# SSM table batches in finer steps beside the first feed-forward, and Toeplitz rows stored by one DMA per group

## The chip, the cores and the metric

One core of a Trainium2 chip runs the whole layer as one program. The metric is the device time of one execution in microseconds. The engines are TensorE (PE, matrix products), VectorE (DVE), ScalarE (ACT), GpSimd (POOL) and SyncE (SP), whose queue issues nearly all DMAs. Each works off its own list in order; they meet at semaphores.

## The reference

One layer on 1024 tokens of width 1024, float32:

```python
h = modulate(rms_norm(x, ffn1_norm), sh1, sc1)
x = x + 0.5 * g1 * swiglu(h, ffn1_w_gate, ffn1_w_up, ffn1_w_down)     # first feed-forward
h = modulate(rms_norm(x, mix_norm), sh2, sc2)
b, c, v, u = split(h @ w_in)
y_conv = short_conv_mixer(b, c, v, conv_w)
y_ssm = s5_mixer(u, lambda, log_dt, b, c, d, glu_w, glu_b)            # 32 groups, 64 states, 16 channels
x = x + g2 * (concat(rms_norm(y_conv), rms_norm(y_ssm)) @ w_out)
h = modulate(rms_norm(x, ffn2_norm), sh3, sc3)
x = x + 0.5 * g3 * swiglu(h, ffn2_w_gate, ffn2_w_up, ffn2_w_down)     # second feed-forward
return rms_norm(x, final_norm)
```

The shifts, scales and gates sh, sc, g are nine vectors, silu(cond) @ w_mod + b_mod. The state space model (SSM) `s5_mixer` is a diagonal recurrence over the tokens; the kernel does it in blocks of TAU = 8 tokens, with tables that depend on the weights alone: a block-Toeplitz matrix `mk` (what eight tokens do to each other), `mi` (tokens to state), `mo` (state to tokens) and the rotors `co` and `si`.

## The kernel before, in words

**First feed-forward.** The 22 column tiles of the gate and up matrices are taken two at a time, as groups fa0 to fa10. Groups 1 to 10 are formed by `seven`: seven products of blocks of weights and activations in place of eight. A block has a gate half (g) and an up half (u), each of four `mm3`; an `mm3` is three matmuls of 128x512 (high and low parts of a float32 split). So a group has 14 halves of 12 matmuls. The products gather in six PSUM banks per group, named B, C and A with g or u, as `fa4gB`. Bank B takes the first, third, fifth and seventh block, each added to what is there, and between them DVE or ACT reads it: the result of the fifth block is read by the DVE instructions `fa4gc` and `fa4uc`, before the seventh may start. Bank C takes the second and the fourth block, read by `fa4gu` and `fa4uu`; bank A the sixth (`fa4gt`, `fa4ut`). `fa4X`, `fa4Y`, `fa4Z`, `fa4W` are the group's products and their combinations, which SP stores as `kept4X` and so on.

**Weights.** Blocks come from DRAM to `raw` tiles (three; SP), some have a second one added by a DMA that POOL issues. ACT rounds them to `w` (high part), DVE subtracts (low part, `w<-raw,w`).

**Side work.** `clock.tick()` runs after each `mm3`, and every `clock.period` ticks the generator `side1` is advanced to its next `yield`. It forms combinations of the activations (`combos1`), the SSM base (`ssm_base`, period 4.5), and then, with period BATCH_PERIOD = 5.5, eight batches (`ssm_batch`) of four SSM groups. A batch loads its parameters `prm`, makes `bb`, `cl` and `bl` on DVE, stores `mo`, makes the rotors `rot` and `rott` and stores them, multiplies `cl` and `bl` on PE (`kp`, eight matmuls of 16x128) and transposes `bl` (`tp`), copies both on ACT (`kc`, `mi`), and stores `mi` and the Toeplitz rows from `kc`. `gate1` yields once if a product of `w_mod` is pending: 24 tiles `wm` of 512 KB are loaded into two buffers in turn, and DVE reduces each against silu(cond) (`mod_vector`), which makes the vectors g1, sc2 and sh2.

**What sets the order.** The code is written in this interleaved order, but past the start of the program a scheduler lays out each engine's list, by program order among what it takes to be ready. An instruction may so stand well ahead of its place in the code; the `wm` products do. At run time each list is strictly in order.

**Toeplitz rows.** `mk_d` is (batch, 128 rows, 4 groups x 128). Row block t (16 rows) has t x 16 zeros and then the first 128 - 16 t columns of `kc`. `ssm_base` stores the zeros, 7 blocks x 8 batches = 56 DMAs; a batch stores its rows in 8 DMAs of 64 pieces, from 512 bytes a piece down to 64.

**After it.** `down7` and `last_parts` finish the feed-forward; the mixer follows, where `out_loads` loads `mk` and `mo` of batch b + 1 after the matmuls of batch b, and `states` and `outputs` use them (`px`, `yy`).

Of the kernel before, what the change touches and what calls it, by code (L numbers as in the profile page):

```python
# [13 lines left out]
F32 = mybir.dt.float32  # L14
F32R = mybir.dt.float32r
I32 = mybir.dt.int32
AF = mybir.ActivationFunctionType
ALU = mybir.AluOpType
# [3 lines left out]
P = 128  # L22
# [9 lines left out]
CH = 16  # L32
TAU = 8
# [7 lines left out]
NB = 8  # L41
GB = G // NB
# [186 lines left out]
def hymba_layer(ctx: ExitStack, tc, x_d, xt_d, wm1_d, wmod_d, gu1_d, gs1_d, ds1_d, wl1_d, win_d, wout_d, glu_d, gu2_d, gs2_d, wd2_d, ds2_d, wl2_d, cols_d, cond_d, lam_d, bc_d, out_d):  # L229
# [228 lines left out]
    def mod_fetch(home):  # L458
        if share[0]:
            share[0] -= 1  # L460
            n, b, i = later.pop(0)
            r = home(f"wm{n}_{b}_{i}")
            SP.dma_start(r, wmod_d[n - 2, b, :, i, :])
            fetched.append((n, 2 * b + i, r))
# [327 lines left out]
    st = t2k("st")  # L792
# [211 lines left out]
    mk_d = scratch.tile([NB, P, GB * P], F32, name="mk_d")  # L1004
# [28 lines left out]
    def ssm_base(sb, sb1):  # L1033
# [130 lines left out]
        mk4 = mk_d[:].rearrange("b p (g c) -> p b g c", g=GB)  # L1164
        for t in range(1, TAU):
            for b in range(NB):
                SP.dma_start(
                    mk4[t * CH : (t + 1) * CH, b, :, 0 : t * CH],
                    zero[:, 0 : t * CH].unsqueeze(1).to_broadcast([CH, GB, t * CH]),
                )  # L1170
            yield
        ssm.update(q=qq, tabs=tabs, base=baset, step=step, lam=lam)

    def ssm_batch(b):
        bp = bps[0]
        gs = slice(b * GB, (b + 1) * GB)
        prm = bp.tile([P, 4, GB, CH], F32, tag="prm", name=f"prm{b}")
        SP.dma_start(prm[:], bc_d[b])
# [3 lines left out]
        p1, p2, e1, e2 = ssm["tabs"]  # L1182

        def bt(name):
            return bp.tile([P, 576], F32, tag="bt", name=name, bufs=4)

        def comb(dst, n, lam, src, op, nm):

            t = bt(nm)[:, : GB * n * CH].rearrange("p (g n c) -> p g n c", g=GB, n=n)
            la = [a[:, 0:n, gs].rearrange("p n g -> p g n").unsqueeze(3).to_broadcast([P, GB, n, CH]) for a in lam]  # L1190
            sc = [a.unsqueeze(2).to_broadcast([P, GB, n, CH]) for a in src]
            V.tensor_tensor(out=dst, in0=la[0], in1=sc[0], op=ALU.mult)
            V.tensor_tensor(out=t, in0=la[1], in1=sc[1], op=ALU.mult)
            yield
            V.tensor_tensor(out=dst, in0=dst, in1=t, op=op)

# [3 lines left out]
        SP.dma_start(mo_d[b].rearrange("p (g m) -> p g m", g=GB), cl4[:, :, 1:9, :].rearrange("p g n c -> p g (n c)"))  # L1200
        bl = bt(f"bl{b}")
        bl4 = bl[:, :512].rearrange("p (g n c) -> p g n c", g=GB, n=8)
        yield from comb(bl4, 8, (e1, e2), (bb[:, 0], bb[:, 1]), ALU.add, f"blt{b}")
        if b >= 2:
            yield from gate1()

        def v3(a):
            return a[:, :512].rearrange("p (g m i) -> p g m i", g=GB, m=8)
# [3 lines left out]

        def rotors():

            r, t = bt(f"rot{b}"), bt(f"rott{b}")
            V.tensor_tensor(out=v3(r), in0=st[0], in1=bs[0], op=ALU.mult)
            V.tensor_tensor(out=v3(t), in0=st[1], in1=bs[1], op=ALU.mult)
            yield
            V.tensor_tensor(out=r[:, :512], in0=r[:, :512], in1=t[:, :512], op=ALU.add)
            A.activation(t[64:128, :512], r[64:128, :512], AF.Copy, scale=-1.0)  # L1220
            for half in (slice(0, 64), slice(64, 128)):
                SP.dma_start(co_d[b, half], r[0:64, :512])
            SP.dma_start(si_d[b, 0:64], r[64:128, :512])
            SP.dma_start(si_d[b, 64:128], t[64:128, :512])

        yield from rotors()
        yield

# [8 lines left out]
        if b >= 2:  # L1237
            yield from gate1()
            yield from gate1()
            yield from gate1()  # L1240
        kc = bt(f"kc{b}")
        kc3 = kc[:CH, :512].rearrange("p (g m) -> p g m", g=GB)
        A.copy(kc[:CH, :512], kp[:])
        for g in range(GB):
            V.scalar_tensor_tensor(
                out=kc3[:, g, 0:CH], in0=ident[:CH, :CH], scalar=ssm["lam"][:CH, 3, b * GB + g : b * GB + g + 1], in1=kc3[:, g, 0:CH], op0=ALU.mult, op1=ALU.add
            )
        mk3 = mk_d[b].rearrange("p (g m) -> p g m", g=GB)
        for t in range(TAU):
            SP.dma_start(mk3[t * CH : (t + 1) * CH, :, t * CH :], kc3[:, :, : P - t * CH])  # L1250
        mi = bt(f"mi{b}")
        A.copy(mi[:, :512], tp[:])
        SP.dma_start(mi_d[b], mi[:, :512])
        yield


    def gate1():

        if fetched:
            mod_tile(mod_home)  # L1260
            yield
# [30 lines left out]
    def side1():  # L1292
        yield from combos1()
        clock.period = 4.5
        sb = side_open.enter_context(tc.tile_pool(name="sb", bufs=1, side="right"))
        with tc.tile_pool(name="sb1", bufs=1, side="right") as sb1:
            yield from ssm_base(sb, sb1)
        clock.period = BATCH_PERIOD
        bps.append(side_open.enter_context(tc.tile_pool(name="bp", bufs=1, side="right")))
        mod_home.pool = side_open.enter_context(tc.tile_pool(name="wmp", bufs=1, side="right"))  # L1300
        share[0] = MODS[1]
        for _ in range(2):
            mod_fetch(mod_home)
        for b in range(NB):
            yield from ssm_batch(b)
# [22 lines left out]
    BATCH_PERIOD = 5.5  # L1328
# [495 lines left out]
```

## Time and profile before

| | us |
|---|---|
| runs (three) | 1685.75, 1690.64, 1691.35; median 1690.64 |
| profiled execution | 1691.52, of which the span is 1689.7 |
| PE busy | 1657.2, 98% of the span |
| DVE busy | 1065.5, 63% |
| ACT busy | 676.8, 40% |
| DMA moved | 340.21 MB, mean 201 GB/s |

The rows in the prediction are of these kinds. A row of the page's first part has an engine's busy time, its share of the span and its instructions. A row by stretch has from:to, its length, and for PE, PEld (weight loads), DVE, ACT and POOL the busy time and (x) the instructions, then the granted TensorE clock (1.00 is full), the share of the DMA engines' time and GB/s. A row of a time line has start, duration, engine (SPq is SP's queue, issuing), line, operation and tiles out<-in, shapes and count; in brackets stand the idle time ahead of it and what ended it. A row of waits has who waited for whom, total us, times, the longest. A row of one tile's instructions has min/median/max duration in ns and the first and last start.

### The profile page before, as it was taken

How to read it: one execution, taken by the hardware profiler on the slowest of the kernel's cores; microseconds unless marked ns; L12 is line 12 of the kernel's file. 1: busy time of each engine (PE TensorE's matmuls, PEld its weight loads, DVE VectorE, ACT ScalarE, POOL GpSimd, SP SyncE). 2: the span in 40 equal slices, each digit the busy share in tenths (PEclk: the TensorE clock that was granted, in tenths of full speed). 3: DMA queues.
4: the chain of work that ended last, by engine and by line, in shares of the span. 5: the costliest groups of instructions: out<-in, count | busy, mean ns of one | idle time of the engine just before them, and what ended most of it. 6: DMA issues, size and time to landing. Idle time of an engine off the chain costs nothing.

```text
span 1689.7 us, 20647 instructions
## 1 busy us (share of the span) xinstructions
PE 1657.2 (98%) x7521; PEld 1364.8 (81%) x7521; DVE 1065.5 (63%) x1581; ACT 676.8 (40%) x992; POOL 169.4 (10%) x207
## 2 busy tenths in 40 slices
PE   8999989999999999999999999999999999999997
PEld 5888878878888888787878778888888888888887
DVE  7984787766567758735656848856555655444454
ACT  6654333333454431332214316434444444322234
POOL 2010000001001102100000121000001101010003
PEclk9999999999999999999999999999999999999999
DMA  9477987987898767145653324558887787989812
GB/s 352 136 165 180 263 253 210 271 235 202 258 315 232 183 210 281 39 112 163 199 158 110 103 97 150 133 140 220 239 227 206 218 222 218 321 271 341 263 55 100
DMA packets 129128, 340.21 MB, mean 201 GB/s; under 512 B 22401, under 2 KB 38017, under 8 KB 128002
## 3 DMA queue, kind: packets, MB, share of 16 engines
q1 hardware_dynamic: 112898, 280.16, 47.9%
q0 software_dynamic: 16128, 58.73, 20.1%
q8 instruction: 59, 0.97, 0.2%
q14 instruction: 43, 0.35, 0.1%
HBM read 254.41 MB, written 76.02 MB: 196 GB/s over the span
## 4 chain that ended last, share of the span: by engine, by line
PE 70%; DVE 7%; DMA 6%; issue 2%; SPq 1%; ACT 0%; POOL 0%; DVEq 0%; POOLq 0%; ACTq 0%
PE fald L111 4%; PE wo L111 3%; PE fad_0B L111 3%; PE fbd_0B L111 3%; PE fad_1B L111 3%; PE fbd_1B L111 3%; PE fb10d L111 2%; PE u L111 2%; PE b L111 2%; DMA wm<-in_wmod 2%; DMA swx<-X 2%; PE c L111 1%; DMA raw<-in_gs 1%; PE fad_0C L111 1%; PE fb0u L111 1%
## 5 line engine op out<-in xcount | busy, mean ns | idle before, releaser
L111 DVE TENSOR_TENSOR w<-raw,w 128x1024 fp32r<-128x1024 f32 x242 | 296.3, 1226 | 264.2 <-ACT w L111 263.9
L111 ACT CAST w<-raw 128x1024 fp32r<-128x1024 f32 x242 | 254.0, 1051 | 310.9 <-DMA raw<-in_ds 60.2
L173 POOL DMA_DIRECT2D raw<-in_gs x80 | 70.6, 885 | 741.9 <-DVE w L111 454.0
L111 DVE CUSTOM_DVE_ANT_0 wm<-wm,cact 128x1024 f32<-128x1024 f32 x56 | 76.0, 1370 | 36.3 <-DMA wm<-in_wmod 31.6
L173 POOL DMA_DIRECT2D raw<-in_ds x32 | 28.1, 877 | 281.4 <-DVE w L111 178.6
L111 PE MATMUL p<-h,w 128*128 128x512 f32 x192 | 49.4, 407 | 1.3 <-ACT h L111 1.0
L111 PE MATMUL wo<-oa,w 128*128 128x512 f32 x192 | 45.5, 391 | 2.9 <-ACT w L111 2.2
L111 PE MATMUL wo<-ob,w 128*128 128x512 f32 x192 | 45.6, 392 | 1.1 <-ACT ob L111 0.6
L111 PE MATMUL v<-h,w 128*128 128x512 f32 x192 | 46.0, 393 | 0.0
L111 PE MATMUL c<-h,w 128*128 128x512 f32 x192 | 46.0, 393 | 0.0
L111 PE MATMUL b<-h,w 128*128 128x512 f32 x192 | 45.1, 392 | 0.0
L111 PE MATMUL u<-h,w 128*128 128x512 f32 x192 | 44.8, 392 | 0.2 <-DVE h L111 0.2
L111 PEld LDWEIGHTS wo<-oa,w 128*128 128x128 f32 x192 | 35.8, 188 | 11.1 <-ACT w L111 2.6
L111 PEld LDWEIGHTS p<-h,w 128*128 128x128 f32 x192 | 35.7, 192 | 9.6 <-ACT h L111 1.6
L111 PEld LDWEIGHTS wo<-ob,w 128*128 128x128 f32 x192 | 35.7, 188 | 9.2 <-ACT ob L111 1.0
L111 PEld LDWEIGHTS u<-h,w 128*128 128x128 f32 x192 | 35.7, 188 | 8.3 <-DVE h L111 0.6
L111 PEld LDWEIGHTS b<-h,w 128*128 128x128 f32 x192 | 35.7, 188 | 7.2
L111 PEld LDWEIGHTS v<-h,w 128*128 128x128 f32 x192 | 35.5, 188 | 7.1
L111 PEld LDWEIGHTS c<-h,w 128*128 128x128 f32 x192 | 35.5, 188 | 7.0
L111 DVE SCALAR_TENSOR_TENSOR x<-fb10d,gate,x 128x512 f32<-128x512 f32 (+1 forms) x20 | 12.9, 643 | 24.4 <-PE fb10d L111 24.3
L111 DVE TENSOR_TENSOR X<-co,X 128x512 f32<-128x512 f32 x8 | 5.5, 692 | 35.3 <-DMA swx<-X 27.5
L111 PE MATMUL fb10d<-fb9lA,w 128*128 128x512 f32 (+1 forms) x120 | 25.6, 347 | 0.0
(1532 smaller groups left out, 3866.5 us busy)
## 6 DMA issues: line engine op xcount, KB each, us to landing
raw<-in_gs SPq DMA_DIRECT2D x80, 512.0 KB, 4.9
raw<-in_gs POOLq DMA_DIRECT2D x80, 512.0 KB, 6.6
wm<-in_wmod SPq DMA_DIRECT2D x56, 512.0 KB, 6.8
raw<-in_ds SPq DMA_DIRECT2D x32, 512.0 KB, 5.9
raw<-in_ds POOLq DMA_DIRECT2D x32, 512.0 KB, 7.3
mw<-in_wm SPq DMA_DIRECT2D x8, 1024.0 KB, 8.9
raw<-in_win SPq DMA_DIRECT2D x16, 512.0 KB, 4.3
raw<-in_wl SPq DMA_DIRECT2D x10, 512.0 KB, 4.3
```

Source lines behind the costliest of these rows:

```text
L111: r = getattr(self.engine, name)(*args, **kw)
L173: self.G.dma_start(out=r[:], in_=src, accum_op=ALU.add)
```

## The change

- `ssm_batch` has more `yield`s: 12 steps a batch instead of 5 in the first two, 16 instead of 9 in the others, and BATCH_PERIOD is 2.75 instead of 5.5.
- `kp` and `tp` come some steps after `bl`, with `gate1` between; the rotors are formed before them and stored after them.
- `prm` of batch b + 1 is loaded in the middle of batch b (`prm_load`).
- `mk_d` gets rows of 256 places, with the 128 wanted ones ahead, and one view (`mk_steps`) shifts block t by 16 t places, so that one DMA per group stores all eight shifted copies (four per batch, 128 pieces of 512 bytes each); what runs over falls into the places between. The zeros take 7 DMAs.

```diff
@@ -1001,7 +1001,10 @@
 
     cact_d = scratch.tile([P, 1024], F32, name="cact_d")
     SP.dma_start(cact_d[:], cact[:])
-    mk_d = scratch.tile([NB, P, GB * P], F32, name="mk_d")
+    mk_row = NB * GB * 2 * P
+    mk_all = scratch.tile([P * mk_row + P], F32, name="mk_d")
+    mk_d = mk_all[: P * mk_row].rearrange("(p b g m) -> b p g m", p=P, b=NB, g=GB)[:, :, :, :P]
+    mk_steps = mk_all[:].rearrange("(t r) -> t r", t=TAU)[:, : CH * mk_row].rearrange("t (c b g m) -> b c t g m", c=CH, b=NB, g=GB)[:, :, :, :, :P]
     mi_d = scratch.tile([NB, P, GB * P], F32, name="mi_d")
     mo_d = scratch.tile([NB, P, GB * P], F32, name="mo_d")
     co_d = scratch.tile([NB, P, GB * P], F32, name="co_d")
@@ -1161,25 +1164,29 @@
             yield
         zero = sb1.tile([CH, 112], F32, name="zero")
         V.memset(zero[:], 0.0)
-        mk4 = mk_d[:].rearrange("b p (g c) -> p b g c", g=GB)
+        mk4 = mk_all[: P * mk_row].rearrange("(p q m) -> p q m", p=P, q=NB * GB)
         for t in range(1, TAU):
-            for b in range(NB):
-                SP.dma_start(
-                    mk4[t * CH : (t + 1) * CH, b, :, 0 : t * CH],
-                    zero[:, 0 : t * CH].unsqueeze(1).to_broadcast([CH, GB, t * CH]),
-                )
+            SP.dma_start(
+                mk4[t * CH : (t + 1) * CH, :, 0 : t * CH],
+                zero[:, 0 : t * CH].unsqueeze(1).to_broadcast([CH, NB * GB, t * CH]),
+            )
             yield
         ssm.update(q=qq, tabs=tabs, base=baset, step=step, lam=lam)
+
+    def prm_load(b):
+        ssm["prm"] = bps[0].tile([P, 4, GB, CH], F32, tag="prm", name=f"prm{b}")
+        SP.dma_start(ssm["prm"][:], bc_d[b])
 
     def ssm_batch(b):
         bp = bps[0]
         gs = slice(b * GB, (b + 1) * GB)
-        prm = bp.tile([P, 4, GB, CH], F32, tag="prm", name=f"prm{b}")
-        SP.dma_start(prm[:], bc_d[b])
+        gated = b >= 2
+        prm = ssm["prm"]
         bb = bp.tile([P, 2, GB, CH], F32, tag="bb", name=f"bb{b}")
         q = tuple(ssm["q"][:, i, gs].unsqueeze(2).to_broadcast([P, GB, CH]) for i in range(2))
         cmul(bp, bb[:], prm[:, 0:2], q, [GB, CH], f"bb{b}")
         p1, p2, e1, e2 = ssm["tabs"]
+        yield
 
         def bt(name):
             return bp.tile([P, 576], F32, tag="bt", name=name, bufs=4)
@@ -1190,18 +1197,22 @@
             la = [a[:, 0:n, gs].rearrange("p n g -> p g n").unsqueeze(3).to_broadcast([P, GB, n, CH]) for a in lam]
             sc = [a.unsqueeze(2).to_broadcast([P, GB, n, CH]) for a in src]
             V.tensor_tensor(out=dst, in0=la[0], in1=sc[0], op=ALU.mult)
+            yield
             V.tensor_tensor(out=t, in0=la[1], in1=sc[1], op=ALU.mult)
             yield
             V.tensor_tensor(out=dst, in0=dst, in1=t, op=op)
+            yield
 
         cl = bt(f"cl{b}")
         cl4 = cl[:].rearrange("p (g n c) -> p g n c", g=GB, n=9)
         yield from comb(cl4, 9, (p1, p2), (prm[:, 2], prm[:, 3]), ALU.add, f"clt{b}")
         SP.dma_start(mo_d[b].rearrange("p (g m) -> p g m", g=GB), cl4[:, :, 1:9, :].rearrange("p g n c -> p g (n c)"))
+        if b + 1 < NB:
+            prm_load(b + 1)
         bl = bt(f"bl{b}")
         bl4 = bl[:, :512].rearrange("p (g n c) -> p g n c", g=GB, n=8)
         yield from comb(bl4, 8, (e1, e2), (bb[:, 0], bb[:, 1]), ALU.add, f"blt{b}")
-        if b >= 2:
+        if gated:
             yield from gate1()
 
         def v3(a):
@@ -1209,22 +1220,15 @@
 
         bs = [a[:, gs, :].unsqueeze(2).to_broadcast([P, GB, 8, 16]) for a in ssm["base"]]
         st = [ssm["step"][:, i, :, gs].rearrange("p m g -> p g m").unsqueeze(3).to_broadcast([P, GB, 8, 16]) for i in range(2)]
-
-        def rotors():
-
-            r, t = bt(f"rot{b}"), bt(f"rott{b}")
-            V.tensor_tensor(out=v3(r), in0=st[0], in1=bs[0], op=ALU.mult)
-            V.tensor_tensor(out=v3(t), in0=st[1], in1=bs[1], op=ALU.mult)
-            yield
-            V.tensor_tensor(out=r[:, :512], in0=r[:, :512], in1=t[:, :512], op=ALU.add)
-            A.activation(t[64:128, :512], r[64:128, :512], AF.Copy, scale=-1.0)
-            for half in (slice(0, 64), slice(64, 128)):
-                SP.dma_start(co_d[b, half], r[0:64, :512])
-            SP.dma_start(si_d[b, 0:64], r[64:128, :512])
-            SP.dma_start(si_d[b, 64:128], t[64:128, :512])
-
-        yield from rotors()
-        yield
+        r, t = bt(f"rot{b}"), bt(f"rott{b}")
+        V.tensor_tensor(out=v3(r), in0=st[0], in1=bs[0], op=ALU.mult)
+        yield
+        V.tensor_tensor(out=v3(t), in0=st[1], in1=bs[1], op=ALU.mult)
+        yield
+        V.tensor_tensor(out=r[:, :512], in0=r[:, :512], in1=t[:, :512], op=ALU.add)
+        yield
+        if gated:
+            yield from gate1()
 
         kp = sm([CH, 512], f"kp{b}")
         for g in range(GB):
@@ -1234,25 +1238,30 @@
         tp = sm([P, 512], f"tp{b}")
         for g in range(GB):
             T.transpose(tp[:, g * P : (g + 1) * P], bl[:, g * P : (g + 1) * P], ident[:])
-        if b >= 2:
-            yield from gate1()
-            yield from gate1()
+        A.activation(t[64:128, :512], r[64:128, :512], AF.Copy, scale=-1.0)
+        for half in (slice(0, 64), slice(64, 128)):
+            SP.dma_start(co_d[b, half], r[0:64, :512])
+        SP.dma_start(si_d[b, 0:64], r[64:128, :512])
+        SP.dma_start(si_d[b, 64:128], t[64:128, :512])
+        yield
+        if gated:
             yield from gate1()
         kc = bt(f"kc{b}")
         kc3 = kc[:CH, :512].rearrange("p (g m) -> p g m", g=GB)
         A.copy(kc[:CH, :512], kp[:])
+        mi = bt(f"mi{b}")
+        A.copy(mi[:, :512], tp[:])
+        yield
         for g in range(GB):
             V.scalar_tensor_tensor(
                 out=kc3[:, g, 0:CH], in0=ident[:CH, :CH], scalar=ssm["lam"][:CH, 3, b * GB + g : b * GB + g + 1], in1=kc3[:, g, 0:CH], op0=ALU.mult, op1=ALU.add
             )
-        mk3 = mk_d[b].rearrange("p (g m) -> p g m", g=GB)
-        for t in range(TAU):
-            SP.dma_start(mk3[t * CH : (t + 1) * CH, :, t * CH :], kc3[:, :, : P - t * CH])
-        mi = bt(f"mi{b}")
-        A.copy(mi[:, :512], tp[:])
+        for g in range(GB):
+            SP.dma_start(mk_steps[b][:, :, g, :], kc3[:, g, :].unsqueeze(1).to_broadcast([CH, TAU, P]))
         SP.dma_start(mi_d[b], mi[:, :512])
         yield
-
+        if gated:
+            yield from gate1()
 
     def gate1():
 
@@ -1299,8 +1308,10 @@
         bps.append(side_open.enter_context(tc.tile_pool(name="bp", bufs=1, side="right")))
         mod_home.pool = side_open.enter_context(tc.tile_pool(name="wmp", bufs=1, side="right"))
         share[0] = MODS[1]
+        prm_load(0)
         for _ in range(2):
             mod_fetch(mod_home)
+        yield
         for b in range(NB):
             yield from ssm_batch(b)
 
@@ -1325,7 +1336,7 @@
             norm_into(act2, h, n2[h], 1, "h2")
 
     movs["B"] = es1.enter_context(tc.tile_pool(name="movB1", bufs=12))
-    BATCH_PERIOD = 5.5
+    BATCH_PERIOD = 2.75
     first_open = ExitStack()
 
     def first_opened():
```

**What moves: DVE, group 4.** The list of DVE from `fa4gu` (C bank of the fourth block) to `fa4gc` (B bank of the fifth). `ISA wm_...` is a reduction of a `w_mod` tile, into `gate` (g1), `scl` (sc2) or `mods` (sh2), and the short `ISA gate` behind it reads out its sum. Before:

```order
L111 TENSOR_TENSOR fa4gu_1814<-fa4gu_1814,fa4gC 128x512
L111 TENSOR_TENSOR gate<-gate,cols 128x8
L111 ISA wm_0_0_2659,scl<-wm_0_0_2659,cact 128x1024
L111 ISA scl 128x1
L111 TENSOR_TENSOR fa4uu_1852<-fa4uu_1852,fa4uC 128x512
L111 TENSOR_SCALAR gate<-gate 128x8
L111 SCALAR_TENSOR_TENSOR fa4Y<-fa4uu_1852,fa4gu_1814 128x512
L111 TENSOR_TENSOR w_1894<-raw_1748,w_1894 128x1024
L111 TENSOR_TENSOR fa4gc_1763<-fa4gc_1763,fa4gB 128x512
```

One `wm` stands between them, the first of sc2. Now, in the same place:

```order
L111 TENSOR_TENSOR fa4gu_1765<-fa4gu_1765,fa4gC 128x512
L111 ISA wm_2_1_3023,scl<-wm_2_1_3023,cact 128x1024
L111 ISA scl 128x1
L111 ISA wm_3_0_3134,scl<-wm_3_0_3134,cact 128x1024
L111 ISA scl 128x1
L111 TENSOR_TENSOR fa4uu_1792<-fa4uu_1792,fa4uC 128x512
L111 SCALAR_TENSOR_TENSOR fa4Y<-fa4uu_1792,fa4gu_1765 128x512
L111 TENSOR_TENSOR w_1839<-raw_1713,w_1839 128x1024
L111 ISA wm_3_1_3192,scl<-wm_3_1_3192,cact 128x1024
L111 ISA scl 128x1
L111 TENSOR_TENSOR fa4gc_1728<-fa4gc_1728,fa4gB 128x512
```

Three stand there, the last of sc2: the reductions have moved up. Of the 24, before and now, there are 1 and 2 ahead of `fa3gu`, 7 and 11 from there to `fa4gu`, 6 and 9 to `fa5gu`, and 10 and 2 behind it.

**PE, the second `kp`, in group 5.** Before, inside the up half of the second block:

```order
L111 MATMUL fa5uC<-h1S_2_723,w_2000 128x512 x3
L111 MATMUL kp_2135<-cl_2017,bl_2043 16x128 x4
L111 MATMUL tp_2140<-ident,bl_2043 128x128 x4
L111 MATMUL fa5uC<-h1S_3_736,w_2000 128x512 x3
L111 MATMUL fa5gB<-h1S_0_747,w_2052 128x512 x3
```

Now, between the fourth and the fifth block:

```order
L111 MATMUL fa5uC<-h1S_2_830,w_2034 128x512 x3
L111 MATMUL fa5uC<-h1S_3_843,w_2034 128x512 x3
L111 MATMUL kp_2149<-cl_2026,bl_2069 16x128 x4
L111 MATMUL tp_2154<-ident,bl_2069 128x128 x4
L111 MATMUL fa5gB<-h1S_0_852,w_1880 128x512 x3
```

`kp` and `tp` stand 17 rows later; nothing else on PE moves than the eight pairs of them. The third block's weights are `w_2052` before and `w_1973` now.

**SP, the stores of group 3.** `kept3...` are the group's products, `co_d` and `si_d` the rotors. Before:

```order
L111 DMA wm_2_0_2375<-in_wmod 128x1024
L111 DMA raw_1641<-in_gs 128x1024
L111 DMA kept3X<-fa3X 128x1024
L111 DMA co_d<-rot_1902 64x512 x2
L111 DMA kept3Y<-fa3Y 128x1024
L111 DMA si_d<-rot_1902 64x512
L111 DMA kept3Z<-fa3Z 128x1024
L111 DMA kept3W<-fa3W 128x1024
L111 DMA si_d<-rott_1903 64x512
L111 DMA raw_1748<-in_gs 128x1024
L111 DMA wm_2_1_2408<-in_wmod 128x1024
```

Now:

```order
L111 DMA wm_0_0_2696<-in_wmod 128x1024
L111 DMA kept3X<-fa3X 128x1024
L111 DMA raw_1634<-in_gs 128x1024
L111 DMA wm_0_1_2750<-in_wmod 128x1024
L111 DMA kept3Y<-fa3Y 128x1024
L111 DMA kept3Z<-fa3Z 128x1024
L111 DMA wm_1_0_2867<-in_wmod 128x1024
L111 DMA kept3W<-fa3W 128x1024
L111 DMA raw_1713<-in_gs 128x1024
L111 DMA wm_1_1_2919<-in_wmod 128x1024
```

The rotors of batch 0 are stored earlier, and loads of `wm` stand between the group's stores, four and not two in this stretch.

## The prediction

> **What bounds the kernel now.** I read the page's first two parts, then the waits of PE, then busy time by stretch, and last the time lines of PE, DVE and SP around the holes.
>
> ```profile
> span 1689.7 us, 20647 instructions
> PE 1657.2 (98%) x7521; PEld 1364.8 (81%) x7521; DVE 1065.5 (63%) x1581; ACT 676.8 (40%) x992; POOL 169.4 (10%) x207
> ```
>
> PE is busy for 98% of the span, so a change on the side work can give back only holes of PE. In the first feed-forward the stretches below (span, PE busy, PEld, DVE, ACT, POOL, granted clock, DMA share, GB/s) hold nearly all of them.
>
> ```profile
> 60.00:200.00 140.00, 140.00 (x619) 115.86 (x619) 103.66 (x194) 68.58 (x105) 14.36 (x48) 1.00 0.71 181
> 220.00:240.00 20.00, 18.89 (x89) 15.08 (x88) 17.43 (x34) 7.83 (x12) 1.78 (x2) 1.00 0.80 224
> 240.00:260.00 20.00, 16.72 (x80) 13.51 (x79) 13.78 (x23) 7.22 (x11) 0.89 (x1) 1.00 0.84 263
> 340.00:360.00 20.00, 17.93 (x78) 14.37 (x78) 16.32 (x31) 5.79 (x9) 2.64 (x3) 0.91 0.84 208
> 360.00:640.00 280.00, 279.93 (x1250) 230.26 (x1249) 189.56 (x267) 124.64 (x182) 22.05 (x25) 1.00 0.83 237
> ```
>
> PE's time line names the three holes: idle time and releaser stand in brackets.
>
> ```profile
> 237.03 2.60 PE L111 MATMUL fa5gC<-h1S,w 128*128 128x512 f32 x10 [1.11 <-DVE w L111]
> 244.95 1.03 PE L111 MATMUL kp<-cl,bl 128*16 128x128 f32 x8 [3.28 <-DVE bl L111]
> 352.55 4.57 PE L111 MATMUL fa7gB<-h,w 128*128 128x512 f32 x12 [2.06 <-DVE fa7gc L111]
> 359.69 2.88 PE L111 MATMUL fa8gB<-h,w 128*128 128x512 f32 x12
> ...
> 240.00:245.00 5.00, 1.72 (x9) 1.14 (x8) 5.00 (x9) 0.30 (x1) 0.89 (x1) 1.00 0.99 328
> 245.00:250.00 5.00, 5.00 (x28) 4.09 (x29) 3.66 (x8) 1.54 (x3) 0.00 (x0) 1.00 1.02 266
> ```
>
> All three are waits for DVE. The last cost more than its 2.06 us: its twelve matmuls took 4.57 us where twelve start 2.72 us after twelve elsewhere (rows of group 4 below), 1.85 us more, at a lower clock:
>
> ```profile
> 351.00:354.00 3.00, 1.45 (x4) 1.21 (x5) 2.97 (x13) 1.56 (x2) 0.88 (x1) 0.78 0.33 52
> 354.00:357.00 3.00, 3.00 (x11) 2.37 (x10) 3.00 (x5) 0.00 (x1) 0.00 (x0) 0.66 0.96 178
> ```
>
> So the holes are worth 1.11 + 3.28 + 2.06 + 1.85 = 8.30 us. That is the most that the change can gain here.
>
> **Why DVE is late.** DVE runs in order, and the 24 products of `wm` stand in its row. Each waits for a 512 KB load into one of two buffers.
>
> ```profile
> 209.51 1.23 DVE L111 CUSTOM_DVE_ANT_0 wm<-wm,cact 128x1024 f32<-128x1024 f32 x1 [5.46 <-DMA wm<-in_wmod]
> 215.12 1.23 DVE L111 CUSTOM_DVE_ANT_0 wm<-wm,cact 128x1024 f32<-128x1024 f32 x1 [1.69 <-DMA wm<-in_wmod]
> 223.16 1.23 DVE L111 CUSTOM_DVE_ANT_0 wm<-wm,cact 128x1024 f32<-128x1024 f32 x1 [0.88 <-DMA wm<-in_wmod]
> 230.34 1.23 DVE L111 CUSTOM_DVE_ANT_0 wm<-wm,cact 128x1024 f32<-128x1024 f32 x1 [1.60 <-DMA wm<-in_wmod]
> 237.57 1.21 DVE L111 CUSTOM_DVE_ANT_0 wm<-wm,cact 128x1024 f32<-128x1024 f32 x1
> ```
>
> These five use the same buffer: from 209.51 to 237.57 are four rounds of 7.0 us (5.6 the shortest, 8.0 the longest), and with two buffers that is one `wm` each 3.5 us.
>
> **The change, part by part.**
>
> *Holes closed: -8.30 us.* The 3.28 us hole is the second `kp`, whose `bl` DVE had not made; in the change it stands 17 rows of three matmuls later (a quarter of 2.72 us each, 11.6 us). The hole of group 7 goes since no `wm` is left there: the order puts all 24 before `fa5uc`, where before ten came after the fourteenth at 237.57. The 1.11 us comes from the same late DVE; its price returns in the next term.
>
> *`wm` packed into groups 3 to 5: +6.7 us.* This is what speaks against the change. Between `fa3gu` and `fa4gu` stood 7 of them, now 11; up to `fa4gc` 8, now 14; and 19 up to `w_1973`, the weights of the third block of group 5. The anchors are:
>
> ```profile
> 172.93 0.68 DVE L111 TENSOR_TENSOR fa3gu<-fa3gu,fa3gC 128x512 f32<-128x512 f32 x1
> ...
> 190.18 2.88 PE L111 MATMUL fa4gB<-h,w 128*128 128x512 f32 x12
> 192.90 2.88 PE L111 MATMUL fa4uB<-h,w 128*128 128x512 f32 x12
> 224.42 2.88 PE L111 MATMUL fa4gB<-h,w 128*128 128x512 f32 x12
> 229.86 2.88 PE L111 MATMUL fa5gB<-h,w 128*128 128x512 f32 x12
> ```
>
> Half a block takes PE 2.72 us. The last block of group 4 adds to the bank that `fa4gc` reads; without `kp` ahead of it it starts 12 halves after 190.18, at 222.8. By pace DVE is done with `fa4gc` at 172.93 + 0.6 + 14 x 3.5 + 0.6 = 223.1: 0.3 us late, where it now has room (the row of the last block starts at 224.42 with no wait). The third block of group 5 starts 4 halves after 229.86, at 240.7. DVE passes the nineteenth `wm` at 173.5 + 66.5 = 240.0 and then has these, with `clt` as long as `cl`, 3.7 us in all:
>
> ```profile
> 233.63 0.34 DVE L111 TENSOR_TENSOR bb<-bb,bb 128x64 f32<-128x64 f32 x2
> 234.50 0.74 DVE L111 TENSOR_TENSOR cl<-tab,prm 128x576 f32<-128x576 f32 x1
> 239.39 0.67 DVE L111 TENSOR_TENSOR fa4Y<-fa4uB,fa4c 128x512 f32<-128x512 f32 x1
> 240.59 1.21 DVE L111 TENSOR_TENSOR w<-raw,w 128x1024 fp32r<-128x1024 f32 x1
> ```
>
> So 243.7, 3.0 us late. To this comes SP's order, for loads are issued in a row too:
>
> ```profile
> 191.78 1.22 DVE L111 CUSTOM_DVE_ANT_0 wm<-wm,cact 128x1024 f32<-128x1024 f32 x1
> ...
> 194.85 0.33 SPq L111 DMA_DIRECT2D kept3Y<-fa3Y  x1
> 202.27 2.13 SPq L111 DMA_DIRECT2D wm<-in_wmod  x2
> ```
>
> The buffer free at 193.0 got its load only at 202.27, 9.3 us later, behind the four stores of group 3 and the rotors. In the change single loads stand between these stores, and one waits behind two of the five that wait on DVE results (Y and Z): I take two fifths, 3.7 us, between 0 and 9.3. Together 6.7 us, the likeliest because both rows lie in the same place of the program. At 2.8 us a piece (the shortest round) the 19 come 13 us earlier and nothing is late; at 4.0 it is 9.5 us more, 16.2.
>
> *Clock after a hole: +0.9 us.* The hole of 2.06 us cost 1.85 us of clock, that of 3.28 us none (granted clock 1.00 in its two stretches, 240 to 250). For one or two new holes I take half of 1.85, between 0 and 3.7. The Trainium skill, "TensorE: Matmul & The Clock Gate", section "What's actually happening", lets the clock fall to half after an idle window of about 3.4 us that runs freely; the trace has it fall after a shorter hole and not after a longer one. By that rule one window at half rate would be an estimated 1.7 us, and the sum would be 1691.6 instead of 1690.8.
>
> *DVE steps, and the tables' other moves.* The products and sums are the same, cut into more steps. What changes is where they stand: batch 0's thirteen instructions from `bb` to `rot`, 0.1 to 0.7 us each and about 6 us together, go from behind `fa3gu` to ahead of it, where DVE idles now:
>
> ```profile
> 159.31 1.23 DVE L111 TENSOR_TENSOR w<-raw,w 128x1024 fp32r<-128x1024 f32 x1 [2.45 <-ACT w L111]
> 164.75 1.23 DVE L111 TENSOR_TENSOR w<-raw,w 128x1024 fp32r<-128x1024 f32 x1 [4.21 <-ACT w L111]
> 170.63 1.23 DVE L111 CUSTOM_DVE_ANT_0 wm<-wm,cact 128x1024 f32<-128x1024 f32 x1 [4.66 <-DMA raw<-in_gs]
> ```
>
> These waits are 11.3 us and cover it: 0 us. If they shrank as well, the 6 us would make DVE later in group 4; the slow end holds that. `prm` is loaded a batch ahead and the rotors' stores are issued a step later; no wait of PE hangs on either, and the rotors are read only in the mixer: 0. A `kc` tile is reused when its stores have landed, which DVE waited for before too:
>
> ```profile
> DVE blt L111 <- DMA mk_d<-kc: 4.5, 1, 4.5
> ```
>
> In groups 6 to 9 such a wait fits into the three halves (8.2 us) between a bank's last product and the next that adds to it, once no `wm` stands there: 0, at most 4.5.
>
> *Stores.* 56 zero stores become 7 and 64 Toeplitz stores 32; what each cost SP:
>
> ```profile
> L111 SPq DMA_DIRECT2D mk_d<-kc x64: 317/592/2037, 232.4 to 447.8; - x64
> L111 SPq DMA_DIRECT2D mk_d<-zero x56: 550/592/1534, 91.8 to 160.9; - x56
> L111 SPq DMA_DIRECT2D mk<-mk_d x8: 325/326/581, 621.3 to 866.6; - x8
> L111 SPq DMA_DIRECT2D ub<-u_d x8: 425/432/489, 754.3 to 851.9; - x8
> ```
>
> About 49 x 0.59 + 32 x 0.59 = 48 us of SP, but PE has no hole before 200 and the raw loads behind them were not what ended the waits that are left: 0 us, a gain only as a faster pace. The rows are whole now, 112 KB more per batch, 0.9 MB. Later `mk` is read in 512 pieces like `ub` and not in 128, 0.11 us more of SP each; it is loaded one batch ahead of its matmul, so 0, at most 8 x 0.11 = 0.9.
>
> Sum against the profiled execution, 1691.52 us (span 1689.7 and 1.8 around it; 0.9 over the median of 1690.64): 1691.5 - 8.3 + 6.7 + 0.9 = 1690.8, said as **1691 us**.
>
> **The rivals.** *The loads keep pace* (0.25): fewer DMAs in the queue, rounds near the 5.6 us seen once. At 3.2 us a piece the 19 come 5.7 us earlier, 1.0 us stays late: 1691.5 - 8.3 + 1.0 = 1684 to 1685. For it speak the shortest round and 80 fewer issues; against it the mean of the rounds, and that those stores do not lie in the stretch of the five rows.
>
> *The loads are the new bound* (0.28, the other side): at 4.0 us a piece PE waits 16.2 us in groups 4 and 5, with clock 1691.5 - 8.3 + 16.2 + 0.9 = 1700. It decides from 3.8 us on (6.7 + 19 x 0.3 = 12.4, net +5). For it: 8.0 us rounds exist, and with the stores of groups 3 and 4 among them loads slow down; against: only the rounds next to busy stretches were so long.
>
> *`kp` still waits* (0.05): its `bl` follows `w_1973` (243.7 + 3.7 with SP's term) by nine instructions of some 6 us, so it is there at 253.4, while PE comes at 229.86 + 8 x 2.72 = 251.6 plus the 6.7 that it has lost, 258.3. Only a wait of DVE for the first batch's stores, as the 4.5 us above, and a little more would open the hole of 3.28 us again: 1694.
>
> **How the numbers follow.** Forecast 0.42, and with `kp` 0.47 within 0.3% (5.1 us, about what the measurement can tell); faster 0.25; slower 0.28. The range goes from all holes closed and none new, 1683, to pace 4.0 with both clock dips, 1703. The forecast's own range is 1686 to 1696.
>
> **What would show it.** Right: no wait of PE for `bl`; no hole after group 5 and PE 280 of 280 there; holes of 3 to 8 us in groups 4 and 5 that end on DVE `w` or `fa4gc`; `wm` 24 times before about 260 with DVE waiting on its load; loads at about 3.5 us each. Wrong: PE full in groups 4 and 5 (pace faster), or waits over 12 us there (slower); a hole in groups 6 to 9 or a longer wait for `mk` in the mixer would be a cost that I set to nothing.

## The result, and the profile after

The changed kernel takes 1711.36 us (median of four runs, 1707.69 to 1715.46) against 1689.97 for the kernel before on the same chip: ratio 1.0131, 95% interval 1.0102 to 1.0161. It is 1.3% slower; the forecast was no change. The profiled execution took 1711.33 us. Of all executions behind the tables here one, 4158.44 us of `orderB_again`, was in the slow state and is left out. Its page begins:

```profile
span 1709.6 us, 20563 instructions
...
PE 1665.5 (97%) x7521; PEld 1370.4 (80%) x7521; DVE 1068.2 (62%) x1581; ACT 676.9 (40%) x992; POOL 170.1 (10%) x207
```

The span is 19.9 us longer. From 150 us to the end of the first feed-forward PE waits six times, and none of the three holes of before is among them:

```profile
186.26 3.00 PE L111 MATMUL fa3gB<-h,w 128*128 128x512 f32 x12 [1.49 <-DVE fa3gc L111]
191.92 4.61 PE L111 MATMUL fa3uB<-h,w 128*128 128x512 f32 x12 [2.66 <-DVE fa3uc L111]
209.07 2.56 PE L111 MATMUL fa4gB<-h1S,w 128*128 128x512 f32 x10 [1.19 <-DVE w L111]
238.67 5.46 PE L111 MATMUL fa4gB<-h,w 128*128 128x512 f32 x12 [8.00 <-DVE scl L111]
286.66 5.40 PE L111 MATMUL fa5gB<-h,w 128*128 128x512 f32 x12 [4.01 <-DVE fa5gc L111]
...
503.93 0.79 PE L111 MATMUL fad_0C<-fa1lS,w 128*128 128x512 f32 x1 [3.36 <-DVE w L111]
```

`scl` in the fourth row is only the small instruction behind `fa4gc` on DVE; it is `fa4gc` that this block of PE needs. By stretch, in the columns used for before:

```profile
180.00:200.00 20.00, 15.85 (x62) 12.29 (x61) 14.10 (x23) 5.32 (x7) 1.75 (x2) 0.91 0.92 236
200.00:220.00 20.00, 18.81 (x83) 15.27 (x82) 12.00 (x20) 7.32 (x10) 0.88 (x1) 1.00 0.94 297
220.00:240.00 20.00, 12.00 (x51) 9.65 (x50) 13.31 (x21) 3.01 (x4) 1.75 (x2) 0.85 0.88 256
...
280.00:300.00 20.00, 15.99 (x60) 12.71 (x59) 15.54 (x28) 5.57 (x8) 1.48 (x2) 0.83 0.81 223
300.00:480.00 180.00, 180.00 (x826) 147.24 (x825) 115.21 (x183) 71.23 (x100) 14.97 (x17) 1.00 0.81 221
500.00:520.00 20.00, 16.64 (x68) 13.35 (x67) 14.18 (x20) 13.17 (x22) 0.87 (x1) 0.91 0.81 251
```

The holes of groups 3 to 5 are 17.35 us. By the prediction's measure (twelve matmuls take 2.72) the clock cost 1.89 + 2.74 + 2.68 = 7.3 more after the three long ones. Less the 8.30 that closed, that is +16.4. The first product of the down part, `fad_0B`, starts at 494.5 where before it was 478.7: +15.8. The down part has another hole of 3.36 and a low clock behind it, and takes 4.5 us longer. From there on nothing is lost: `fald`, the last part, starts 20.3 later, and the end is 19.9 later.

On DVE's time line stand the start of batch 0, the two instructions that the prediction had anchored, two of the waits for `wm`, and a wait that it had bounded at 4.5 (the profile names no releaser; batch 0's last store from `kc` lands at 267.61):

```profile
169.38 0.49 DVE L111 TENSOR_TENSOR bb<-prm,qq 128x128 f32<-128x128 f32 x2 [5.98 <-DMA kept2W<-fa2W]
...
180.24 0.69 DVE L111 TENSOR_TENSOR fa3gu<-fa3gu,fa3gC 128x512 f32<-128x512 f32 x1
...
190.03 1.23 DVE L111 CUSTOM_DVE_ANT_0 wm<-wm,cact 128x1024 f32<-128x1024 f32 x1 [3.92 <-DMA wm<-in_wmod]
...
218.53 1.23 DVE L111 CUSTOM_DVE_ANT_0 wm<-wm,cact 128x1024 f32<-128x1024 f32 x1 [4.82 <-DMA wm<-in_wmod]
...
237.84 0.68 DVE L111 TENSOR_TENSOR fa4gc<-fa4gc,fa4gB 128x512 f32<-128x512 f32 x1
...
267.69 0.69 DVE L111 TENSOR_TENSOR blt<-tab,bb 128x512 f32<-128x512 f32 x1 [4.00 <-issue]
```

`fa3gu` is 7.3 us later than before (172.93), and `fa4gc`, done at 238.44, is 15.3 later than the pace of the forecast had it (223.1). From the start of the one to the start of the other are 57.6 us and 14 `wm`; less 0.6 for `fa3gu` that is 4.07 us a piece, where the forecast took 3.5. SP's time line shows where the other 8.0 us lie:

```profile
180.73 1.57 SPq L111 DMA_DIRECT2D si_d<-rot  x1
182.40 0.66 SPq L111 DMA_DIRECT2D si_d<-rott  x1
183.10 16.63 SPq L111 DMA_DIRECT2D wm<-in_wmod  x6
...
207.91 0.33 SPq L111 DMA_DIRECT2D kept3Y<-fa3Y  x1
210.25 0.33 SPq L111 DMA_DIRECT2D kept3Z<-fa3Z  x1
210.62 2.30 SPq L111 DMA_DIRECT2D wm<-in_wmod  x1
213.02 1.04 SPq L111 DMA_DIRECT2D kept3W<-fa3W  x1
...
214.61 5.51 SPq L111 DMA_DIRECT2D wm<-in_wmod  x2
```

The buffer of the load at 183.10 was free at 179.18, that of the load at 210.62 at 207.27, that of the one at 214.61 at 211.96 (the ends of the reductions before). These three, and the load right behind the first, went out 0.8 to 3.9 us late: they stood behind the rotors' stores and behind `kept3Y`, `kept3Z` and `kept3W`, stores of results of DVE. The other ten of the 14 went out within 0.1 us. A round, from one reduction to the next in the same buffer, is 10.0 to 12.5 us for the four and 5.5 to 7.9 for the ten, 6.8 in the mean, close to the 7.0 of the forecast. The late ones also landed slowly: 6.9 to 7.9 us where the landing is recorded, against 4.1 to 6.6. With the four issued at once and all landing times as they were, `fa4gc` would come 4.4 us earlier; that is an estimate from this row of DVE, no run has it.

### The profile page after: what moved, and what is told of

The parts are those of the page before. It is cut to its first block, busy times and chain, and to the rows that moved or that the text cites. A ratio compares the mean times of both kernels' runs of the same rounds, so it can differ in the third digit from the quotient of the medians.

```text
span 1709.6 us, 20563 instructions
## 1 busy us (share of the span) xinstructions
PE 1665.5 (97%) x7521; PEld 1370.4 (80%) x7521; DVE 1068.2 (62%) x1581; ACT 676.9 (40%) x992; POOL 170.1 (10%) x207
## 3 DMA queue, kind: packets, MB, share of 16 engines
q0 software_dynamic: 16128, 58.73, 19.9%
## 4 chain that ended last, share of the span: by engine, by line
PE 73%; DVE 10%; DMA 9%; issue 4%; ACT 2%; SPq 1%; POOL 0%; DVEq 0%; POOLq 0%; ACTq 0%
DMA wm<-in_wmod 4%; PE fald L111 3%; PE fbd_1B L111 3%; PE fbd_0B L111 3%; PE p L111 3%; PE fb10d L111 2%; PE fad_1B L111 2%; PE fad_0B L111 2%; PE wo L111 2%; PE b L111 2%; DVE w L111 2%; PE u L111 2%; DMA swx<-X 2%; PE fad_0C L111 1%; PE fad_1C L111 1%
```

## The experiments

Four theories were at stake. **P**: the `wm` products, packed ahead of what PE needs and paced by their loads. **S**: finer steps and batch 0 ahead of `fa3gu`. **D**: the store DMAs. **Q**, added after the first four runs: the order of POOL's adding loads. For all kernels, in us; the starts are PE's first matmul of that name in each trace, the ratios are to the kernel before run beside it:

```
kernel         median   ratio [95%]                 wm ahead of     starts of                   fad_0B
                                                    fa4gc  fa5gc   fa5gB  fa6gB  fa8gB  fad_0B  to fald
before         1689.97  -                               9     14   229.9  275.9  359.7   478.7    152.9
after          1711.36  1.0131 [1.0102, 1.0161]        16     23   248.3  294.6  375.5   494.5    157.4
stores         1697.29  1.0061 [1.0039, 1.0083]        15     19   242.1  284.8  364.1   483.1    153.4
steps          1710.87  1.0125 [1.0098, 1.0152]        12     19   238.8  285.9  368.0   487.0    162.4
quarter        1699.58  1.0069 [1.0042, 1.0096]        20     24   240.0  279.6  360.5   479.5    159.3
b0             1699.79  1.0052 [1.0037, 1.0066]        17     21   241.6  281.3  362.2   481.1    157.8
addorder       1705.53  1.0083 [1.0067, 1.0099]        16     23   244.3  290.7  371.6   490.5    152.6
nowm_add       1688.51  0.9985 [0.9974, 0.9995]         -      -   229.9  269.6  350.5   469.5    159.4
inorder        1686.14  0.9977 [0.9963, 0.9991]         0      0   230.0  269.7  350.6   471.3    156.2
inorder_add    1684.22  0.9968 [0.9957, 0.9980]         0      0   229.2  268.8  349.7   469.5    156.9
inorderB_add   1694.59  1.0021 [1.0008, 1.0033]         0      0   229.5  270.8  350.1   469.1    158.7
orderB_again   1692.82  1.0023 [1.0011, 1.0035]         0      0   229.0  270.3  349.6   470.0    161.9
stores_order   1693.55  1.0019 [1.0006, 1.0033]         0      1   229.5  270.8  350.1   469.1    164.7
steps_order    1691.40  1.0015 [1.0003, 1.0027]         0      0   229.5  269.1  350.0   469.2    160.8
```

From `fald` to the start of `fb1gB` in the second feed-forward the traces take 441.8 to 447.7 us, with the same lists; a median is held against its trace only that closely.

**One part of the change alone.** `stores` is the kernel before with the new `mk_d`, 7 zero stores and `mk_steps`:

```diff
-            for b in range(NB):
-                SP.dma_start(
-                    mk4[t * CH : (t + 1) * CH, b, :, 0 : t * CH],
...
-        for t in range(TAU):
-            SP.dma_start(mk3[t * CH : (t + 1) * CH, :, t * CH :], kc3[:, :, : P - t * CH])
+        for g in range(GB):
+            SP.dma_start(mk_steps[b][:, :, g, :], kc3[:, g, :].unsqueeze(1).to_broadcast([CH, TAU, P]))
```

> The kernel before with the new stores alone (7 zero stores, 4 Toeplitz stores a batch); steps and period as before. The scheduler then lays the products of wm earlier all the same: 13 stand ahead of fa4gu where before had 8, and 15 ahead of fa4gc where before had 9 and the change has 16. Theory P (what costs is the packing of wm ahead of the instructions that PE needs): about half to all of the loss, 1700 to 1712 us, with a hole of PE at the last block of group 4 that ends on DVE. Theory S (finer steps and batch 0 ahead of fa3gu cost): no loss, 1684 to 1692. Theory D (the store DMAs themselves cost on their queue): 1700 to 1712 as well, but with no hole on DVE behind wm in group 4.

`steps` is the other half, the changed kernel with those lines turned back.

> The changed kernel with the stores of before (56 zero stores, 8 Toeplitz stores a batch). 12 of the wm stand ahead of fa4gc (the change 16, before 9) and 21 ahead of fa5Z (24, 16). Theory P: four wm of 3.9 us less ahead of fa4gc, so that the hole of 8.0 us there nearly goes: 1690 to 1700. Theory S: as slow as the change, 1708 to 1715. Theory D: as fast as before or faster, 1683 to 1691.

Measured: 1697.29 and 1710.87. The holes of PE, first of `stores`, then of `steps`:

```profile
190.14 4.53 PE L111 MATMUL fa3uB<-h,w 128*128 128x512 f32 x12 [2.36 <-DVE fa3uc L111]
234.31 5.22 PE L111 MATMUL fa4gB<-h,w 128*128 128x512 f32 x12 [5.28 <-DVE fa4gc L111]
253.82 1.03 PE L111 MATMUL kp<-cl,bl 128*16 128x128 f32 x8 [1.32 <-DVE bl L111]
```

```profile
229.08 5.46 PE L111 MATMUL fa4gB<-h,w 128*128 128x512 f32 x12 [5.66 <-DVE fa4gc L111]
278.27 5.01 PE L111 MATMUL fa5gB<-h,w 128*128 128x512 f32 x12 [5.06 <-DVE fa5gc L111]
...
529.72 1.65 PE L111 MATMUL fad_1B<-fa1lA,w 128*128 128x512 f32 x3 [3.74 <-DVE fad_1c L111]
```

The stores alone lose 7 us, somewhat less than P had said, in the hole that P named and D did not; S, which allowed no loss, does not explain it. Nothing but DMA issues was changed in that kernel, and yet the scheduler put six more `wm` ahead of `fa4gc`. In `steps` P missed by 11 us: with only 12 ahead of `fa4gc` the hole is nearly as long. DVE had passed `fa3gu` at 172.69 there and `fa4gc` came at 228.25, so (55.6 - 0.6) / 12 = 4.6 us a piece, slower than with the new stores: the first of them starts only at 179.23, and four of their loads go out 1.9 to 3.4 us after their buffer is free. The number is S's; whether its cause is S's the next runs tell. Half of the 18.2 us that the span is longer than before's lies in the down part (162.4 us against 152.9).

**The products spread, and left out.** `inorder` keeps each `wm` behind the DVE instruction ahead of it in the code:

```diff
-        if "mixed" in pools:
-            V.follow(r, widened[-1] if pools["mixed"] else before)
+        V.follow(r, widened[-1] if pools.get("mixed") else before)
```

> The changed kernel with one order added: each product of wm stays behind the DVE instruction that the code has ahead of it. None then stands ahead of fa5gu, 8 ahead of fa7gu, 24 ahead of fa10gu; batch 0 and the stores are as in the change. Theory P: no hole of PE in groups 3 to 5, 1680 to 1688, or a few us more if the hole of 3.4 us in the down product stays. Theories S and D: at least half of the loss stays, 1700 or more.

`nowm_add` leaves the 24 out (constants stand for the three vectors), and has POOL's order of `addorder` below:

```diff
-        share[0] = MODS[1]
+        for _ in range(24):
+            later.pop(0)
+        V.memset(gate[:, 0], 0.5)
...
```

> The changed kernel without the 24 wm loads and products in the first feed-forward (three of the nine vectors are constants instead), POOL's adding loads in code order. Theory P: no hole of PE in groups 3 to 9, 1679 to 1686. Theory S or D: what finer steps, batch 0 ahead of fa3gu and the new stores cost stays, 1690 or more.

Measured: 1686.14 and 1688.51. Neither has a hole of PE in groups 3 to 5, with the finer steps, the new stores and batch 0 ahead of `fa3gu` all in place (in `inorder` `fa3gu` comes at 178.75, and nothing waits). So S and D fall as causes of the loss in the groups, and P stands: group 8 starts at 350.6 and 350.5 with the products spread or gone, at 375.5 with them packed. `inorder` lies in its range. `nowm_add` is 2.5 us above its own: the holes that are left are in the down part, 4.85 us, which P does not speak of.

**Pace and start of the packed row.** `quarter` loads 256 of the 1024 columns; the product keeps its length:

```diff
-            SP.dma_start(r, wmod_d[n - 2, b, :, i, :])
+            if "mixed" in pools:
+                SP.dma_start(r, wmod_d[n - 2, b, :, i, :])
+            else:
+                SP.dma_start(r[:, :QL], wmod_d[n - 2, b, :, i, :QL])
```

> The changed kernel with a quarter of each wm load (256 of 1024 columns) in the first feed-forward; the product of full length runs over silu(cond) alone, so the three vectors are other numbers. The 24 stand even earlier (18 ahead of fa4gu, 20 ahead of fa4gc), each with its full time on DVE. Theory P in its load form (the pace of the 512 KB loads into two buffers): the holes of groups 3 to 5 go, 1680 to 1690. If DVE's own time for the wm (24 x 1.2 us) is what makes it late: holes as large as in the change or larger, 1708 or more.

`b0` runs batch 0 with DVE's instructions tied into code order:

```diff
+            yield from in_code_order(ssm_batch(b)) if b == 0 else ssm_batch(b)
-            yield from ssm_batch(b)
```

> The changed kernel with batch 0's DVE instructions kept in code order, that is behind fa4gu and not ahead of fa3gu; the wm products fill the place (4 ahead of fa3gu, 17 ahead of fa4gc). Theory P: the wm are paced by their loads, so the 17th comes at most 2 us earlier than the 16th in the change, and the hole at the last block of group 4 stays: 1706 to 1713. If it is batch 0's six us ahead of fa3gu that makes DVE late: 1703 or less.

Measured: 1699.58 and 1699.79. The first lies between the two answers that were offered; the second missed P's answer and lies in the one set against it, 1703 or less. The loads by line (number, size, median us from issue to landing), between 160 and 300 in `after` and in `quarter`:

```profile
wm<-in_wmod SPq DMA_DIRECT2D x24, 512.0 KB, 6.3
```

```profile
wm<-in_wmod SPq DMA_DIRECT2D x24, 128.0 KB, 3.2
```

and the holes of `quarter` and then of `b0` in the groups:

```profile
187.51 4.57 PE L111 MATMUL fa3gB<-h,w 128*128 128x512 f32 x12 [3.12 <-DVE fa3gc L111]
231.24 4.41 PE L111 MATMUL fa4gB<-h,w 128*128 128x512 f32 x12 [3.78 <-DVE fa4gc L111]
```

```profile
188.27 4.58 PE L111 MATMUL fa3gB<-h,w 128*128 128x512 f32 x12 [3.37 <-DVE fa3gc L111]
232.74 4.52 PE L111 MATMUL fa4gB<-h,w 128*128 128x512 f32 x12 [4.51 <-DVE fa4gc L111]
```

In `quarter` 18 products lie between `fa3gu` (178.26) and `fa4gc` (230.41): (52.2 - 0.6) / 18 = 2.86 us a piece in place of 4.07. DVE's waits for the loads add up to 10.5 us there, against 20.3 in `after`, but the four products more are 4.9 us of DVE's own time. So the loads set the pace in part only, and the holes are more than halved, not gone. "The holes go" was wrong for that reason.

In `b0` the sixteenth product is done at 223.0, 3.7 us a piece behind `fa3gu` (178.45); from there DVE works without a wait up to `fa4gc` (231.91), on `cl` and `bl` of batch 0 among others. The first `wm` is reduced at 168.65, not at 176.21, and I had thought of 170.6 and two us of gain; and the rotors' stores, which now come later, hold up none of the loads behind `fa3gu`. `fa4gc` comes 5.9 us earlier, the hole shrinks from 8.00 to 4.51, and the one of group 5 is gone. So the start of the row and the stores of batch 0 count as well as the loads' own time; what S had said of batch 0 is a part of the loss after all, though only beside a packed row, since `inorder` has batch 0 ahead of `fa3gu` without a hole.

**POOL's adding loads.** Behind the start, the trace shows where 5.98 us of waiting came from. Some blocks of weights are a sum: SP loads one part and POOL issues a second load that adds to it. Around the end of group 2 POOL's time line reads, before and after:

```profile
134.93 0.89 POOL L173 DMA_DIRECT2D raw<-in_gs  x1 [15.48 <-DMA mk_d<-zero]
138.99 0.88 POOL L173 DMA_DIRECT2D raw<-in_gs  x1 [3.17 <-DVE w L111]
144.74 0.88 POOL L173 DMA_DIRECT2D raw<-in_gs  x1 [4.87 <-DVE w L111]
```

```profile
138.86 1.78 POOL L173 DMA_DIRECT2D raw<-in_gs  x2 [19.47 <-DVE w L111]
152.67 0.87 POOL L173 DMA_DIRECT2D raw<-in_gs  x1 [12.03 <-DVE w L111]
```

Two adding loads have changed places in POOL's list. The one now in front has to wait for DVE to have done with its buffer, and the one behind it, which could go at 134.9, goes with it at 138.9. ACT waits for them:

```profile
149.96 1.05 ACT L111 CAST w<-raw 128x1024 fp32r<-128x1024 f32 x1 [10.04 <-DMA raw<-in_gs]
```

then DVE's `w` for ACT, and the third adding load for DVE, 7.9 us late; behind it come `fa2W`, its store, and behind that store in SP's queue `prm` and the first `wm`. The same swap stands ahead of the down part:

```profile
462.18 0.88 POOL L173 DMA_DIRECT2D raw<-in_ds  x1 [19.35 <-DMA fa1lS<-kept1Z]
465.50 0.89 POOL L173 DMA_DIRECT2D raw<-in_ds  x1 [2.44 <-DVE w L111]
473.07 0.89 POOL L173 DMA_DIRECT2D raw<-in_ds  x1 [6.67 <-DVE w L111]
```

```profile
481.43 1.79 POOL L173 DMA_DIRECT2D raw<-in_ds  x2 [22.75 <-DVE w L111]
495.32 0.89 POOL L173 DMA_DIRECT2D raw<-in_ds  x1 [12.10 <-DVE w L111]
```

before and after again (after is 15.8 us later on PE here, so the first of the two is 3.4 late and the third 6.4). `addorder` ties POOL's adding loads into code order and changes nothing else by hand:

```diff
     def add(self, r, src):
-        self.G.dma_start(out=r[:], in_=src, accum_op=ALU.add)
+        got = self.G.dma_start(out=r[:], in_=src, accum_op=ALU.add)
+        if getattr(self, "added", None) is not None:
+            self.V.follow(got, self.added)
+        self.added = got
```

> The changed kernel with one order added: POOL issues its adding loads (the second weight block added onto a raw tile) in the order of the code. In the change the first two of the down product stand the other way round, as a scheduler's choice. Nothing differs ahead of the end of group 10. Theory Q (that swap makes the third adding load late and so opens the hole of 3.4 us at fad_0C): the hole goes and some clock with it, 1705 to 1708 us. If the hole comes from the last batch's stores, which run later there: no difference, 1709 to 1713.

Measured: 1705.53, inside Q's range, 5.8 us below the change. The expectation overlooked that the swap at the end of group 2 is undone too. The holes that are left:

```profile
204.39 3.60 PE L111 MATMUL fa4gB<-h1S,w 128*128 128x512 f32 x10 [2.86 <-DVE w L111]
234.83 5.28 PE L111 MATMUL fa4gB<-h,w 128*128 128x512 f32 x12 [7.24 <-DVE scl L111]
282.94 5.13 PE L111 MATMUL fa5gB<-h,w 128*128 128x512 f32 x12 [4.27 <-DVE fa5gc L111]
```

The hole at `fad_0C` is gone, and the down part is 4.8 us shorter. With DVE's list unchanged there, `fa3gu` is at 174.48, not 180.24: of the 7.3 us of late start 5.8 came from POOL's order. PE gains only 4.0 in the groups, since the packed row makes it wait again in group 4.

**Both orders, and what else is needed.** `inorder_add` has the lines of `inorder` and of `addorder`; `inorderB_add` is the kernel before with the same lines; `orderB_again` is that kernel once more for a second profile; `stores_order` and `steps_order` are the two halves above with both orders.

> The kernel before (old steps, old stores, kp straight behind bl) with the two orders alone: each wm product behind its DVE predecessor in the code, and POOL's adding loads in code order. None of the wm stands ahead of fa5gu, 10 ahead of fa7gc. Theory P: this order is all that made the ordered variant fast, so 1683 to 1688, no waits for wm in groups 4 to 7; the wait of kp for bl (3.28 us) may stay. If the finer steps, the later kp or the new stores carry the gain: 1689 or more.

> The changed kernel with both orders: wm products behind their DVE predecessors in the code, and POOL's adding loads in code order. Theory: the late start of batch 0 and the hole at fad_0C both come from POOL's swaps, the holes of groups 4 and 5 from the packed wm; with both gone 1682 to 1687 us, at or a little below the 1686.1 of the wm order alone, and below before. If POOL's order does not matter once the wm are spread: 1685 to 1688.

> The kernel before with both orders once more, for a second profile. The first gave a median of 1694.6 over twelve runs, and its profile was of the fastest (1688.6). If kp straight behind bl costs in the usual run, the profile shows PE waits for bl in groups 4 to 9, 3 us or more; if the clock after short waits in the mixer makes the spread, it shows the same waits as the first at a lower granted clock.

> The kernel before with the new stores and both orders; kp straight behind bl and coarse steps as before. If the new stores carry the gain that the ordered change has over the ordered kernel before: 1683 to 1688. If the finer steps and the later kp carry it: 1691 to 1696, as the ordered kernel before.

> The changed kernel with the old stores (56 zero stores, 8 a batch) and both orders. If finer steps and the later kp carry the gain: 1683 to 1688. If the new stores carry it: 1691 to 1696.

Measured: 1684.22 for `inorder_add`, as its theory said, and the lowest median here: 0.9968 of before, 0.9957 to 0.9980. That interval overlaps the one of `inorder`, so POOL's order is not shown to gain anything once the products are spread. The kernel before does not gain from the two orders (1694.59 and 1692.82), so P's word that the order alone makes `inorder` fast was wrong. Nor does either half (1693.55, 1691.40), so each of the two runs gave the answer "the other half carries it", and together they contradict both: with the 24 spread, only the kernels with both the new stores and the finer steps gain (`inorder`, `inorder_add`). All of those with both orders reach `fad_0B` at 469 to 470, some nine us earlier than before. They give much of it back in the down part, or all, as in `orderB_again`:

```profile
484.54 1.22 PE L111 MATMUL fad_0B<-fa1lS,w 128*128 128x512 f32 x2 [3.07 <-ACT fad_0t L111]
...
514.79 0.96 PE L111 MATMUL fad_1B<-fa1lA,w 128*128 128x512 f32 x3 [2.19 <-DVE fad_1c L111]
```

There are no waits for `bl` in either profile of that kernel, so `kp` straight behind `bl` is not what it pays for once the `wm` are spread. Nor is it the mixer: from `fald` to `fb1gB` both profiles take 444.7 us, and they differ in the down part (158.7 and 161.9). There `before` has 0.07 us of idle PE at a granted clock of 1.00, and `orderB_again` 5.8 us at 0.98, which together make about its 9 us more. Why these waits come when PE is at `fad_0B` some nine us earlier no run shows: the down part is long without any `wm` (159.4), and with POOL's loads in code order (156.9). That stays open, and so does why the new stores and the finer steps gain only together. A kernel that is at `fad_0B` at 469.5 and then takes 152.6 would by these figures be 4 us faster than `inorder_add`.

## Why the prediction was wrong

- *Holes closed, -8.30*: right. All three are gone, and from 300 to 480 PE is busy 180.00 of 180.00.
- *`wm` packed, +6.7*: the right mechanism at the right place, and mis-sized: 17.35 us of holes. Two of its inputs failed, the start (the next point) and what the stores in SP's queue cost (the one on SP below). Its pace of 3.5 held where a load went out at once: 6.8 us a round. On the whole packing did not lengthen the landing either: between 160 and 300 the median is 6.3 us, in the kernel before 6.2. The Trainium skill, "DMA: Bandwidth & Descriptors", section "Anatomy of one DMA", has a fixed 2.0 us and the bytes at 436 GB/s, for the path that POOL's loads take; as an estimate that is 3.2 us for 512 KB. The medians of 3.2 and 6.3 us of 128 and 512 KB loads here (SP's path, in the busy stretch) give, as an estimate, a fixed part near that, 2.2, but 127 GB/s for the rest.
- *The anchor `fa3gu` at 172.93, batch 0 "0 us"*: this step failed. It was at 180.24, 7.3 of the 15.3 us. The prediction had named a shrinking cover as the slow end; it went by DVE's and SP's lists there and left out POOL's, which is where 5.8 of it came from. `fa3uB` and `fa3gB` waited in group 3, where no hole was forecast.
- *Third block of group 5, 3.0 late*: it did not wait. PE itself was by then 18 us late; the hole of group 5 is at the seventh block. There `fa5gc` stands behind the 23rd `wm`, whose load went out at 276.78, 21.4 us after its buffer was free, behind the stores of group 4 and of batches 0 and 1. The 4.00 us wait of `blt`, set at 0 for groups 6 to 9, fell into group 5 too, ahead of the rotors whose stores hold up that load; what it cost there no run tells apart.
- *SP's two fifths, 3.7*: the right kind of term, and too small. In the row up to `fa4gc` the four rounds with late loads cost 8.0 us: 4.4 for the late issue by the estimate above, the rest with the slower landing beside the stores, which no run tells apart. It had counted waits behind Y and Z of group 3; the longest, 3.9 us, was behind the rotors of batch 0, which now are stored ahead of these loads.
- *Clock, +0.9*: 7.3 us in the groups, since there were three long holes and not one, and each cost 1.9 to 2.7.
- *Stores, 0 us*: wrong of the kernel, whatever SP's time was worth. With the new stores the scheduler laid the products earlier (`stores`, +7 us with nothing else changed by hand).
- *Nothing after group 5*: wrong by 4.5 us, in the down part, by POOL's second swap (152.6 without it, `addorder`). `mk` in the mixer cost nothing, as said: `yy` waits 4.6 us in all against 4.9.
- With these the sum is -8.3 + 17.35 + 7.3 + 4.5 = +20.9, against 19.9 measured in the span (a clock figure counts 0.16 too much each time, since an undisturbed row of twelve shows 2.88 us). The rival "the loads are the new bound", 4.0 us a piece and 16.2 us of holes, comes nearest, and loads did slow down beside the stores. But its 16.2 had no late start in it, so that it is so close to 17.35 is partly luck; and its 1700 lacked the clock and the down part.

## What to carry to other kernels

When a scheduler lays out the lists, taking DMA issues away moves instructions that nobody touched: compare the list of every engine, the one that issues adding loads too, and tie what isn't urgent behind its place in the code (here that turned a loss of 1.3% into a gain of 0.3%). When a row of loads and products is packed closer, follow each load's issue in its queue: what stands ahead of it, and when that can go. Count from when the first load can be issued. Most holes of PE over two microseconds cost about two more in clock here, so count the holes and not only their sum.

## What the runs showed of the hardware

The clock's price depends little on the length of the hole. By twelve matmuls less 2.72 us, holes of 2.36, 3.12, 3.78, 4.01, 4.51, 5.28, 5.66 and 8.00 us cost 1.81, 1.85, 1.69, 2.68, 1.80, 2.50, 2.74 and 2.74 more (the rows above); that of 1.49 cost 0.3. The Trainium skill, "TensorE: Matmul & The Clock Gate", section "What's actually happening", lets the clock fall after one idle window of about 3.4 us that runs freely, and keeps it down for one: as an estimate 1.7 us. The price agrees at its lower end. The threshold does not: holes of 2.06, 2.36 and 2.66 us were followed by a lower clock, while that of 2.19 us in the down part of `orderB_again` was not (granted clock 1.00 from 512 to 530), nor the 3.28 us ahead of `kp` in the kernel before. What decides it the runs do not show.
